# Gated DeltaNet layer: the sample's state scaling goes from GpSimd to ScalarE in pieces, the turn of the inverted blocks from ScalarE to VectorE

## The chip, the cores and the metric

The kernel runs on one core of a Trainium2 chip. The metric is device time in microseconds (us) of one launch, the median over several executions. A core has five instruction streams that run side by side and meet at semaphores: TensorE (PE in the profile; PEld are its weight loads), VectorE (DVE), ScalarE (ACT), GpSimd (POOL) and SyncE (SP), which here issues the DMAs. Each stream keeps its own order: an instruction that waits holds up all behind it on its engine.

## What is computed

One inference step of a trunk of two layers with 1024 channels: layer 0 mixes tokens by gated DeltaNet, layer 1 by RWKV-7. There is one prompt of 1024 tokens with 16 learned tokens ahead of it, and a batch of 8 samples of 8 tokens each that carry on from given states. Only the first layer matters here. Cut to that:

```
proj = rmsnorm(x) @ w_in                     # q, k, v, z, b, a
q, k, v = silu(causal_conv(q|k|v, last 3 rows))
q, k = l2norm(q) * 128**-0.5, l2norm(k)      # 8 key heads, each used by 2 of the 16 value heads
beta, g = sigmoid(b), -exp(a_log) * softplus(a + dt_bias)
# in chunks (64 tokens of the prompt, the 8 tokens of a sample), gc = cumsum(g):
A = I + strict_lower((beta k) k^T * decay)   # solved: u, w = A^-1 [beta v, beta k exp(gc)]
v_new = u - w S
o = (q exp(gc)) S + (tril(q k^T) * decay) v_new
S = S * exp(gc_last) + (k exp(gc_last - gc))^T v_new
y = (rmsnorm(o) * silu(z)) @ w_out ;  x = x + y
```

For the samples there are 8 states S of 128x128 for each of the 16 heads, 128 matrices in all. The new states `S * exp(gc_last) + ...` are an output (`out_s_gdn`).

## The kernel before, in words

**Groups.** The 16 value heads are done in 8 groups j = 0..7 of one key head and two value heads. All tokens (samples first, then prompt) stand in 9 tiles of 128, and three column pieces s = 0, 1, 2 of up to 408 columns go through the projection (`product`, matmuls `d..<-xc/xa,whi/wlo`). A weight tile is loaded (`wraw`), rounded by ScalarE into `whi` (L86), and GpSimd forms the remainder `wlo = wraw - whi` (L90); TensorE needs both. ScalarE and VectorE do the convolution (`raw`, `cvy`, `vt`, L523, L529, L543, L547).

**The inverse.** The blocks of a group's A are written to DRAM in 32x32 pieces (`ltd`, L715), read back with one block per partition (`invA`, L726), and inverted row by row on VectorE in 31 steps, each of a product `invtmp<-invA,invT` (L570) and a sum `invT<-invT,invtmp` (L572). `steps` deals these out between other work; `spread` (L737) runs what is left, then turns each inverted block (L740, 72 partitions by 1024 numbers, read with a stride of 32 numbers: `"p i j -> p j i"`) into `invA`, writes the turned blocks to DRAM as `g_u` (L742) and the unturned ones as `g_t` (L743), and reads them back: three DMAs `T1n<-g_t` (L746) and twelve `TT<-g_u` (L753). With `T1n`, TensorE starts the first of four merges (`y32`, matmuls `rY<-T1n,E`), which VectorE copies into `invA` (L764), and three more follow (`rU`, `rY`, `rU`). The write of `g_t` waits for the last inverse step, that of `g_u` for the turn, and both stand ahead of `T1n` in SP's queue.

**The chain.** `gdn_recur` walks over the 9 token tiles of the group: X (L877 to L880) and `rA<-X,TT`, then `w<-rA,nbp` on ScalarE (L62), `rA<-w,ktok` and `rA<-w,attn` on TensorE, S on VectorE (L902), `rA<-S,K` for the next tile, and o (ScalarE L62, VectorE L913). After three tiles the outputs are normalised: `ovar` (VectorE, L1045), `ors` (GpSimd, L102), `on_t` (VectorE, L110 to L112), and `o<-o,ors` on ScalarE (L62, 128x128, scale per partition).

**The sample's states.** For each head, four samples at a time, `sample_states` loads a tile `Sb` of 128x4x128 (L1076). `gdn_sample_scale` (L1098) multiplies the eight states of a head by their decay `eglb`, with one GpSimd instruction of 128x128 each (L1101). `gdn_sample_write` (L1103) adds the matmul results `msw` and `fsw` on VectorE (L1112) and stores the tile (L1113, `out_s_gdn`).

**What sets the order.** `gdn_events` files every piece of work under a slot number (one period of a group is 36 slots); `chain_events` files what belongs to a group's chain relative to the slot a at which the chain begins. TensorE's and ScalarE's instructions stand in the order of these slots. A scheduler orders VectorE, GpSimd and SP by its own estimates, so a change in one place can move other rows there. In the trace, groups 4 to 7 repeat with a period of about 124 us (from 582 us to about 1080 us); groups 0 to 3 lie ahead of that, with longer stretches of the inverse behind one another. Layer 1 follows from about 1260 us.

Of the kernel before, what the change touches and what calls it, by code (L numbers as in the profile page):

```python
# [10 lines left out]
AF = mybir.ActivationFunctionType  # L11
ALU = mybir.AluOpType
# [23 lines left out]
class Builder:  # L36
# [634 lines left out]
    def gdn_prep(self, j, G):  # L671

        nc, t, fp = self.nc, self.t, self.fp
# [58 lines left out]
        def steps(n):  # L732
            with self.tc.issue_after(self.anchor) if self.anchor else ExitStack():
                for _ in range(n):
                    next(G.inv, None)

        def spread():  # L737
            steps(31)
            A, Tv = buf[0][0:72, 0:1024], G.Tv
            nc.scalar.copy(G.Av, Tv.rearrange("p i j -> p j i"))  # L740
            ud, td = self.dram([72, 1024], f"g{j}_u"), self.dram([54, 1024], f"g{j}_t")
            nc.sync.dma_start(ud, A)  # L742
            nc.sync.dma_start(td, Tv[0:54].rearrange("p i j -> p (i j)"))  # L743
            T1 = self.T1n
            for r in range(3):
                nc.sync.dma_start(T1[32 * r:32 * r + 32, :, 32 * (r % 2):32 * (r % 2) + 32],  # L746
                                  td[18 * r:18 * r + 18].rearrange("c (i j) -> i c j", j=32))
            G.TT = [self.TTs[(3 * j + s) % 4] for s in range(3)]
            TT.extend(G.TT)
            for s in range(3):  # L750
                for r in range(4):
                    b = slice(32 * r, 32 * r + 32)
                    nc.sync.dma_start(G.TT[s][b, :, b], ud[18 * r + 6 * s:18 * r + 6 * s + 6].rearrange("c (j i) -> j c i", i=32))  # L753
# [181 lines left out]
    def at(self, u, f, *a):  # L935
        self.events.setdefault(u, []).append(lambda: f(*a))

    def chain_events(self, j, G, a):

        it, Sb, nm = [], {}, {}  # L940
        at = lambda u, *f: self.at(a + u, *f)

        def begin():
            it.append(self.gdn_recur(j, G[j]))
            next(it[0])

        def decay(s):
            if s == 0:
                G[j].at, G[j].kt, G[j].w = [None] * 3, [None] * 9, [None] * 9
            G[j].at[s] = self.decays(j, s, self.gp, "attn", 2)  # L950

        def exps(s, tt):
            self.decay_exps(j, s, G[j].at[s], tt)

        def scores(s):
            self.gdn_scores(j, s, G[j], G[j].at[s])

        def tokens(tg):
            G[j].kt[tg] = self.gdn_tokens(j, G[j], tg)

        def states(h):
            Sb[h] = [self.sample_states(j, h, q) for q in (0, 1)]

        def norm(s):
            nm[s] = self.gdn_norm(j, G[j], s, *G[j].seg[s])
        for s, (u, v, w) in enumerate(((-8.5, -5.6, -2.5), (1.6, 4.3, 6.5), (8.2, 10.3, 12.4))):
            at(u, decay, s)
            for tt in range(3):
                at(v + 0.9 * tt, exps, s, tt)
            at(w, scores, s)  # L970
        at(-4.3, states, 0)
        at(-3.4, lambda: self.gdn_sample_scale(j, 0, Sb[0]))
        at(-1.4, tokens, 0)
        at(-1, begin)
        for x in range(26):
            at(x, lambda: next(it[0]))
            if x % 3 == 1:
                at(x + 1.3, lambda: G[j].squares())
        for tg, u in enumerate((0.4, 3.6, 7.5, 10.5, 13.5, 16.5, 19.5, 22.5)):
            at(u, tokens, tg + 1)  # L980
        at(0.6, lambda: self.gdn_sample_rows(G[j], 0))
        at(2.2, lambda: self.gdn_sample_write(j, 0, G[j], Sb[0]))
        at(2.6, lambda: self.gdn_sample_rows(G[j], 1))
        at(2.7, states, 1)
        at(2.8, lambda: self.gdn_sample_scale(j, 1, Sb[1]))
        at(5.2, lambda: self.gdn_sample_write(j, 1, G[j], Sb[1]))
        for s in range(3):
            at(9 * s + 8.4, norm, s)
            for tt in range(3):
                at(9 * s + 10.2 + 0.5 * tt, lambda s=s, tt=tt: nm[s](tt))  # L990
            for h in (0, 1):
                at((14.5, 23.5, 30.5)[s] + h, lambda s=s, h=h: self.gdn_norm_out(j, G[j], s, h))
# [102 lines left out]
            for b in range(4):  # L1095
                self.nc.gpsimd.tensor_scalar(G.we[:, b], w[0:64], self.bmask4[:, b:b + 1], None, op0=ALU.mult)

    def gdn_sample_scale(self, j, h, Sb):  # L1098
        for g in (0, 1):
            for u in range(4):  # L1100
                self.nc.gpsimd.tensor_scalar(Sb[g][:, u], Sb[g][:, u], self.eglb[:, 2 * j + h, 4 * g + u:4 * g + u + 1], None, op0=ALU.mult)  # L1101

    def gdn_sample_write(self, j, h, G, Sb):  # L1103
        nc = self.nc
# [1437 lines left out]
```

## Time and profile before

| what | us |
|---|---|
| median of three runs | 2224.76 |
| the three runs | 2217.19, 2224.76, 2225.53 |
| the profiled execution | 2228.82 |
| its span in the profile | 2226.8 |
| busy in the span: TensorE, VectorE, ScalarE, GpSimd | 2070.8, 1580.8, 1270.7, 941.9 |
| mean granted TensorE clock | 0.971 |

The profile comes from one execution; 2.0 us of its time lie outside its span. Busy times are sums over an engine's instructions. A row of the timeline gives start, duration, engine, line, what is written from what, the shape and the count, and in brackets how long the engine had been idle and which event released it. A row of the waits gives who waited for whom, the sum, how often, and the longest. In a row of the windows stand, for one stretch, its length, then busy time and instruction count of PE, PEld, DVE, ACT and POOL, then the granted clock, the DMA share and GB/s. A row of a group ends with busy time, mean ns of one, and the idle time ahead of them with its commonest releaser.

### The profile page before, as it was taken

The numbers are of one execution on the slowest core, as the hardware profiler recorded it, in microseconds if no ns is written. First come the engines' busy times: TensorE is split into PE (matmuls) and PEld (weight loads), VectorE is DVE, ScalarE is ACT, GpSimd is POOL, SyncE is SP. The second block draws the span as 40 slices with busy tenths as digits, with TensorE's granted clock in tenths as the row PEclk, the third lists the DMA queues.
The fourth block names the chain that finished last, engine by engine and source line by source line (L and its number), as shares of the span: only waits on it lengthen the run. The fifth ranks groups of instructions, "written<-read, shape, count | busy, mean of one in ns | idle before, by whom it ended". The sixth has DMA issues, their size and how long they took to land. (4 is left out here: it accounts for less than half of the span.)

```text
span 2226.8 us, 54821 instructions
## 1 busy us (share of the span) xinstructions
PE 2070.8 (93%) x20404; PEld 1925.8 (86%) x20404; DVE 1580.8 (71%) x4213; ACT 1270.7 (57%) x3641; POOL 941.9 (42%) x1253
## 2 busy tenths in 40 slices
PE   5979898988999999999899999979899999999997
PEld 5879798888989998989799999968798988888886
DVE  6978868777786978776333585676887747876755
ACT  5436555555555555655633365674755546677774
POOL 3524435453354545444323154244533444444444
PEclk9989999998999999999999999989999999999999
DMA  4423242423333342434525314655566476677864
GB/s 117 117 67 104 67 113 81 104 75 85 99 107 81 88 115 79 104 93 114 169 78 142 86 49 152 221 165 177 163 184 170 122 211 170 191 218 231 237 176 137
DMA packets 430660, 292.64 MB, mean 131 GB/s; under 512 B 147145, under 2 KB 412986, under 8 KB 430394
## 3 DMA queue, kind: packets, MB, share of 16 engines
q1 hardware_dynamic: 430394, 289.14, 45.2%
q8 instruction: 161, 2.64, 0.5%
q14 instruction: 105, 0.86, 0.1%
HBM read 197.68 MB, written 91.37 MB: 130 GB/s over the span
## 5 line engine op out<-in xcount | busy, mean ns | idle before, releaser
L90 POOL TENSOR_TENSOR wlo<-wraw,whi 128x512 fp32r<-128x512 f32 (+1 forms) x246 | 322.4, 1312 | 381.6 <-ACT whi L86 335.0
L76 PE MATMUL d<-xc,whi 128*128 128x384 f32 (+2 forms) x1006 | 278.3, 336 | 1.1 <-DVE xc L312 0.7
L523 DVE SCALAR_TENSOR_TENSOR cvy<-raw,cw,cvy 128x408 f32<-128x408 f32 (+2 forms) x288 | 194.4, 676 | 31.6 <-ACT cvy L62 29.9
L86 ACT CAST whi<-wraw 128x512 fp32r<-128x512 f32 (+1 forms) x246 | 149.8, 611 | 94.6 <-PE d L76 50.5
L76 PEld LDWEIGHTS d<-xc,whi 128*128 128x128 f32 (+1 forms) x1006 | 182.6, 188 | 4.1 <-ACT whi L86 1.2
L76 PE MATMUL d<-xc,wlo 128*128 128x384 f32 (+3 forms) x476 | 157.0, 338 | 3.3 <-POOL wlo L90 3.3
L76 PE MATMUL dv<-xc,whi 128*128 128x384 f32 (+1 forms) x480 | 154.4, 341 | 0.0
L76 PE MATMUL dz<-xc,whi 128*128 128x384 f32 (+1 forms) x480 | 153.5, 338 | 0.0
L76 PE MATMUL d<-xa,whi 128*128 128x384 f32 (+3 forms) x450 | 141.1, 337 | 7.1 <-ACT ev L2342 4.3
L1101 POOL TENSOR_SCALAR Sb<-Sb,eglb 128x128 f32<-128x128 f32 x128 | 112.9, 898 | 74.2 <-DMA Sb<-in_state_gdn 33.9
L62 ACT ACTIVATE o<-rA,gcol 128x128 f32<-128x128 f32 x128 | 42.0, 367 | 132.8 <-DVE S L902 132.5
L570 DVE TENSOR_TENSOR invtmp<-invA,invT 72x31 f32<-72x31 f32 (+15 forms) x248 | 99.3, 400 | 3.4
L76 PE MATMUL dv<-xa,whi 128*128 128x384 f32 (+1 forms) x288 | 99.6, 346 | 0.0
L76 PE MATMUL dz<-xa,whi 128*128 128x384 f32 (+1 forms) x288 | 98.4, 342 | 0.0
L572 DVE TENSOR_TENSOR invT<-invT,invtmp 72x31 f32<-72x31 f32 (+15 forms) x248 | 95.6, 386 | 3.5
L76 PEld LDWEIGHTS d<-xc,wlo 128*128 128x128 f32 (+1 forms) x476 | 89.0, 188 | 7.0 <-POOL wlo L90 3.9
L76 PEld LDWEIGHTS dz<-xc,whi 128*128 128x128 f32 x480 | 89.3, 188 | 5.4 <-issue 5.3
L76 PEld LDWEIGHTS d<-xa,whi 128*128 128x128 f32 (+1 forms) x450 | 83.2, 188 | 11.0 <-ACT ev L2342 4.6
L76 PEld LDWEIGHTS dv<-xc,whi 128*128 128x128 f32 x480 | 90.7, 191 | 1.2 <-issue 1.2
L76 PE MATMUL d<-xa,wlo 128*128 128x384 f32 (+3 forms) x252 | 84.3, 334 | 1.1 <-POOL wlo L90 1.1
L76 PE MATMUL dq<-xc,whi 128*128 128x384 f32 (+1 forms) x240 | 80.2, 351 | 3.0 <-ACT whi L86 3.0
L76 PE MATMUL dk<-xc,whi 128*128 128x384 f32 (+1 forms) x240 | 79.3, 351 | 0.0
(523 smaller groups left out, 6881.6 us busy)
## 6 DMA issues: line engine op xcount, KB each, us to landing
wraw<-in_gdn_w_in SPq DMA_DIRECT2D x96, 256.0 KB
wraw<-in_rwkv_w_rkvz SPq DMA_DIRECT2D x80, 256.0 KB
Sb<-in_state_gdn SPq DMA_DIRECT2D x64, 256.0 KB
sldcak<-cakd SPq DMA_DIRECT2D x24, 576.0 KB
wraw<-in_rwkv_w_o SPq DMA_DIRECT2D x42, 256.0 KB
E<-drow SPq DMA_DIRECT2D x24, 384.0 KB
attn<-drow SPq DMA_DIRECT2D x24, 384.0 KB
wraw<-in_gdn_w_out SPq DMA_DIRECT2D x36, 256.0 KB
```

The costliest lines, as they stand in the source:

```text
L62: return self.nc.scalar.activation(out, in_, func, bias=bias, scale=scale, **kw)
L76: self.nc.tensor.matmul(out, lhsT, rhs, start=start, stop=stop)
L86: nc.scalar.copy(hi, x)
L90: e.tensor_tensor(lo, x, hi.bitcast(F32), op=ALU.subtract)
L523: nc.vector.scalar_tensor_tensor(y[0][:, 0:wd], raw[:, k:k + wd], cw[k], y[0][:, 0:wd], op0=ALU.mult, op1=ALU.add)
L570: nc.vector.tensor_tensor(tmp, A[:, j, j + 1:32].unsqueeze(2).broadcast_to([nb, n, m]), Tv[:, j, 0:m].unsqueeze(1).broadcast_to([nb, n, m] ...
L572: nc.vector.tensor_tensor(Tv[:, j + 1:32, 0:m], Tv[:, j + 1:32, 0:m], tmp, op=ALU.subtract)
L1101: self.nc.gpsimd.tensor_scalar(Sb[g][:, u], Sb[g][:, u], self.eglb[:, 2 * j + h, 4 * g + u:4 * g + u + 1], None, op0=ALU.mult)
```

## The change

Three edits:

1. In `spread`, the turn of the inverted blocks (L740) is a VectorE copy instead of a ScalarE copy. Shape and stride stay the same; there are 8, one for each group.
2. `gdn_sample_scale` takes a piece number k and scales two states of the head, half g = k // 2, with ScalarE (`act` with AF.Identity and a scale per partition) instead of all eight with GpSimd. There are 128 of these in all, as before.
3. The calls are filed as four pieces for each head, at slots a - 0.6, 0.3, 0.7 and 1.4 for the first head and a + 3.4, 3.8, 4.4 and 4.8 for the second, instead of all at a - 3.4 and a + 2.8.

```
-            nc.scalar.copy(G.Av, Tv.rearrange("p i j -> p j i"))
+            nc.vector.tensor_copy(G.Av, Tv.rearrange("p i j -> p j i"))
...
-        at(-3.4, lambda: self.gdn_sample_scale(j, 0, Sb[0]))
+        for k in range(4):
+            at((-0.6, 0.3, 0.7, 1.4)[k], lambda k=k: self.gdn_sample_scale(j, 0, Sb[0], k))
+            at((3.4, 3.8, 4.4, 4.8)[k], lambda k=k: self.gdn_sample_scale(j, 1, Sb[1], k))
...
-        at(2.8, lambda: self.gdn_sample_scale(j, 1, Sb[1]))
...
-    def gdn_sample_scale(self, j, h, Sb):
-        for g in (0, 1):
-            for u in range(4):
-                self.nc.gpsimd.tensor_scalar(Sb[g][:, u], Sb[g][:, u], self.eglb[:, 2 * j + h, 4 * g + u:4 * g + u + 1], None, op0=ALU.mult)
+    def gdn_sample_scale(self, j, h, Sb, k):
+        g = k // 2
+        for u in range(2 * (k % 2), 2 * (k % 2) + 2):
+            self.act(Sb[g][:, u], Sb[g][:, u], AF.Identity, scale=self.eglb[:, 2 * j + h, 4 * g + u:4 * g + u + 1])
```

GpSimd's queue in group 4, before: rows between two weight remainders. `Sb_8486` is the second half of the group's first head, `Sb_8828` the first half of its second head, `wlo_7979` the remainder of a weight tile of the next projection.

```order
L90 TENSOR_TENSOR wlo_7890<-wraw_7752,whi_7889 128x512
L511 COPY raw_7935<-raw_7859 128x3
L1101 TENSOR_SCALAR Sb_8486<-Sb_8486,eglb_124 128x128 x4
L505 MEMSET raw_8054 128x3
L1101 TENSOR_SCALAR Sb_8828<-Sb_8828,eglb_124 128x128 x4
L90 TENSOR_TENSOR wlo_7979<-wraw_7754,whi_7978 128x512
```

The same place of GpSimd's queue now:

```order
L90 TENSOR_TENSOR wlo_7890<-wraw_7752,whi_7889 128x512
L511 COPY raw_7935<-raw_7859 128x3
L505 MEMSET raw_8054 128x3
L90 TENSOR_TENSOR wlo_7979<-wraw_7754,whi_7978 128x512
L513 COPY last_6609<-raw_7935 128x3
```

The eight scalings between the two remainders are gone from this queue.

VectorE's queue at the end of the inverse of group 1, before: the last steps (`72x7x25` to `72x31`) and what stands behind them.

```order
L572 TENSOR_TENSOR invT_2237<-invT_2237,invtmp_2995 72x7x25
L570 TENSOR_TENSOR invtmp_2998<-invA_2235,invT_2237 72x156
L572 TENSOR_TENSOR invT_2237<-invT_2237,invtmp_2998 72x6x26
L570 TENSOR_TENSOR invtmp_3039<-invA_2235,invT_2237 72x135
L572 TENSOR_TENSOR invT_2237<-invT_2237,invtmp_3039 72x5x27
L570 TENSOR_TENSOR invtmp_3042<-invA_2235,invT_2237 72x112
L572 TENSOR_TENSOR invT_2237<-invT_2237,invtmp_3042 72x4x28
L570 TENSOR_TENSOR invtmp_3045<-invA_2235,invT_2237 72x87
L572 TENSOR_TENSOR invT_2237<-invT_2237,invtmp_3045 72x3x29
L570 TENSOR_TENSOR invtmp_3048<-invA_2235,invT_2237 72x60
L572 TENSOR_TENSOR invT_2237<-invT_2237,invtmp_3048 72x2x30
L570 TENSOR_TENSOR invtmp_3051<-invA_2235,invT_2237 72x31
```

The same queue now, its last rows up to the turn and the first merge's copy.

```order
L523 SCALAR_TENSOR_TENSOR cvy_3227<-raw_3159,cw_393,cvy_3227 128x384
L572 TENSOR_TENSOR invT_2237<-invT_2237,invtmp_3045 72x3x29
L529 SCALAR_TENSOR_TENSOR K_3278<-raw_3010,cvy_3126 128x64
L529 SCALAR_TENSOR_TENSOR K_3278<-raw_3010,cvy_3126 128x320
L523 SCALAR_TENSOR_TENSOR cvy_3227<-raw_3159,cw_393,cvy_3227 128x384
L570 TENSOR_TENSOR invtmp_3048<-invA_2235,invT_2237 72x60
L110 TENSOR_TENSOR on_t_3217<-ors_3216 128x6
L504 COPY raw_3961<-histT_2955 128x8x3
L523 SCALAR_TENSOR_TENSOR cvy_3227<-raw_3159,cw_393,cvy_3227 128x384
L572 TENSOR_TENSOR invT_2237<-invT_2237,invtmp_3048 72x2x30
L111 SCALAR_TENSOR_TENSOR on_t_3217<-on_t_3217,ovar_3214 128x6
L570 TENSOR_TENSOR invtmp_3051<-invA_2235,invT_2237 72x31
```

Before, the last seven steps stood behind one another without other work; now convolution (`cvy`, `K`), S, o and norm rows stand between them, and the last step (with L740 right behind it) comes after them. In this stretch the added rows ahead of the last step are six `cvy`, one `vt`, two S, two o, one `bv`, one `qeps`, one `ovar`, two `K`, three of the norm and one copy of `raw`.

ScalarE's queue in group 1, before: the turn stands ahead of the chain's `w`.

```order
L62 ACTIVATE raw_2826<-cvy_2902 128x384
L740 COPY invA_2235<-invT_2237 72x1024
L62 ACTIVATE ojunk_3080,ssq_2749<-o_2883 128x128
L62 ACTIVATE ojunk_3082,ssq_2749<-o_2883 128x128
L543 COPY raw_3010<-dk_3013 128x8x8
L544 COPY raw_3010<-dk_3013 128x320
L62 ACTIVATE w_3029<-rA_3031,nbp_544 128x128
```

And ScalarE's queue now, in group 4, about the second half of the second head (`Sb_8830`); in group 1 the rows above stand without the L740 row.

```order
L62 ACTIVATE Sb_8828<-Sb_8828,eglb_124 128x128 x2
L62 ACTIVATE o_8792<-rA_8797,gcol_123 128x128
L62 ACTIVATE o_8792<-rA_8798,gcol_123 128x128
L62 ACTIVATE E_8712<-E_8712,gcol_123 128x128 x2
L86 CAST whi_8909<-wraw_8679 128x512
L62 ACTIVATE attn_8770<-attn_8770,gcol_123 128x128 x2
L62 ACTIVATE Sb_8830<-Sb_8830,eglb_124 128x128 x4
L62 ACTIVATE E_8712<-E_8712,gcol_123 128x128 x2
```

The four scalings of this half stand between products of decays (`E`, `attn`) on ScalarE, behind the rounding `whi_8909`; before, they stood on GpSimd right ahead of the remainder of that same tile. In groups 4 to 7 VectorE's order ahead of the last inverse step is as before, and L740 stands one `cvy` behind that step. TensorE's order is the same up to the layer's output projection (about 1060 us), where GpSimd, VectorE and SP rows move among one another too.

## Prediction

> **What bounds the kernel now.** The page first, for the engines and the groups that the change touches.
>
> ```profile
> PE 2070.8 (93%) x20404; PEld 1925.8 (86%) x20404; DVE 1580.8 (71%) x4213; ACT 1270.7 (57%) x3641; POOL 941.9 (42%) x1253
> L1101 POOL TENSOR_SCALAR Sb<-Sb,eglb 128x128 f32<-128x128 f32 x128 | 112.9, 898 | 74.2 <-DMA Sb<-in_state_gdn 33.9
> ```
>
> TensorE is the bound at 93%, so an edit on other engines can win only what TensorE stands idle, and the time it runs at half clock. The windows say where that is: groups 0 to 3 in one stretch, then one row for each period.
>
> ```profile
> 60.00:582.00 522.00, 471.40 (x3956) 446.39 (x3956) 408.92 (x1132) 275.90 (x870) 222.38 (x335) 0.95 0.34 93
> 582.00:707.00 125.00, 119.31 (x1024) 113.04 (x1023) 95.93 (x278) 71.69 (x230) 58.57 (x82) 0.99 0.35 95
> 957.00:1082.00 125.00, 115.50 (x991) 108.16 (x990) 85.43 (x222) 73.10 (x240) 59.91 (x82) 0.99 0.42 117
> ```
>
> Groups 0 to 3 leave 522.0 - 471.4 = 50.6 us of TensorE idle and run at a clock of 0.95; a period of the later groups leaves 125.0 - 119.3 = 5.7 us. TensorE's waits name the releasers, first for 60 to 582 us (four rows), then for 582 to 1082 us (two).
>
> ```profile
> PE rY L76 <- DMA T1n<-g_t: 11.2, 5, 10.0
> PE rA L76 <- ACT w L62: 7.5, 1, 7.5
> PE dv L76 <- POOL wlo L90: 6.2, 2, 4.1
> PE f L73 <- DVE vt L529: 4.3, 2, 2.6
> ...
> PE rA L76 <- DVE S L902: 9.2, 8, 2.1
> PE dv L76 <- POOL wlo L90: 7.1, 4, 1.8
> ```
>
> In the later periods it waits once for GpSimd's `wlo` (7.1 us in 4 waits), and most of its waits for S, 9.2 us in 8 with 2.1 the longest, is one wait a period of about 2 us. In the earlier groups it waits for the read of the inverse (`T1n`), once for ScalarE's `w`, twice for `wlo` (4.1 and the remaining 2.1).
>
> **Scalings off GpSimd: the wait for wlo in groups 4 to 7.** GpSimd's rows of group 4, and TensorE's row behind them.
>
> ```profile
> 626.87 4.24 POOL L1101 TENSOR_SCALAR Sb<-Sb,eglb 128x128 f32<-128x128 f32 x4 [1.68 <-PE mktok L73]
> 631.14 4.20 POOL L1101 TENSOR_SCALAR Sb<-Sb,eglb 128x128 f32<-128x128 f32 x4
> 635.31 1.29 POOL L90 TENSOR_TENSOR wlo<-wraw,whi 128x512 fp32r<-128x512 f32 x1
> ...
> 636.65 0.44 PE L76 MATMUL dv<-xc,wlo 128*128 128x384 f32 x1 [1.76 <-POOL wlo L90]
> ```
>
> Eight scalings hold `wlo` until 635.31. Without these 8.4 us it can start 8 us sooner, and the wait of 1.76 us goes whatever else happens. The inverse's steps and S behind it wait for TensorE there, so they come earlier with it. Four periods: -7.0 us.
>
> **The wait for S at the period's end.** GpSimd, SP, VectorE and TensorE, in that order.
>
> ```profile
> 692.10 2.35 POOL L1101 TENSOR_SCALAR Sb<-Sb,eglb 128x128 f32<-128x128 f32 x4 [6.71 <-DVE X L880]
> 694.40 1.32 POOL L90 TENSOR_TENSOR wlo<-wraw,whi 128x512 fp32r<-128x512 f32 x1
> 710.07 1.32 POOL L102 TENSOR_TENSOR ors<-ovar,cvals 128x6 f32<-128x6 f32 x1
> ...
> 695.75 0.39 SPq L425 DMA_DIRECT2D wraw<-in_gdn_w_in  x1
> 699.59 1.12 SPq L1076 DMA_DIRECT2D Sb<-in_state_gdn  x2
> 704.42 0.44 SPq L646 DMA_DIRECT2D attn<-drow  x1
> ...
> 711.43 0.17 DVE L110 TENSOR_TENSOR on_t<-ors 128x6 f32<-128x6 f32 x1 [5.12 <-POOL ors L102]
> ...
> 712.32 0.49 PE L76 MATMUL rA<-S,K 128*128 128x128 f32 x2 [1.99 <-DVE S L902]
> ```
>
> The other four scalings hold the next `wlo` by up to 2.35 us; SP's next weight load waits for that `wlo` to free its buffer (695.75), and behind it in SP's queue stand the stores and loads of the states, `ltd` and `attn<-drow` (704.42). That last transfer feeds GpSimd's rows up to `ors` (710.07), VectorE waits 5.12 us for `ors` with S queued behind, and TensorE waits 1.99 us for S. Take the scalings away and the queue is up to 2.35 us early. The bounds are 0 (the stores of the states wait for ScalarE instead, or a landing of another transfer comes last) and 2.0; since the whole length of this chain moves and I see one link (the landing of the states' store ahead of 699.59) that needn't move, I take 1.0 each: -4.0 us, ends 0 and -8.
>
> Behind that wait the clock falls, behind the wait for `wlo` it doesn't (rows: after the first, then after the second).
>
> ```profile
> 638.00:642.00 4.00, 4.00 (x29) 4.00 (x28) 2.38 (x10) 2.54 (x7) 0.39 (x2) 1.00 0.62 180
> 714.00:718.00 4.00, 4.00 (x18) 4.00 (x17) 3.80 (x11) 3.94 (x17) 1.28 (x1) 0.57 0.25 65
> ```
>
> 18 matmuls instead of 29 in 4 us at a clock of 0.57: 4 x (1 - 0.57) = 1.7 us of work lost in a period. A wait of 1.76 us left the clock whole and one of 1.99 didn't; two rows so close set no safe edge for the 1 us that I leave standing, so I take half of the four: -3.4 us, ends 0 and -6.8. The Trainium skill ("TensorE: Matmul & The Clock Gate", Part 1) has the clock halved after an idle window of about 3.4 us, on windows that run free of the kernel's own times. By it alone the phase decides in each period, and the term could be either end; that two almost equal waits ended differently here agrees with it.
>
> **What ScalarE takes on.** The nearest rows are its own 128x128 scalings with a scale per partition, and the copy that it gives up.
>
> ```profile
> L62 ACT ACTIVATE o<-o,ors 128x128 f32<-128x128 f32 x144 | 48.4, 397 | 23.5 <-DVE ors L112 23.4
> L740 ACT COPY invA<-invT 72x1024 f32<-72x1024 f32 x8 | 16.5, 2065 | 28.2 <-DVE invT L572 28.2
> ```
>
> 128 scalings at 48.4 / 144 = 0.34 us of busy time are 43 us, 16.5 us go: +26.5 us on an engine that is busy 71.7 of 125 us in a period. Each place takes 0.7 to 1.4 us. Two of a group's four tiles were there at 626.87 already; the last is scaled on GpSimd from 692.10 and stands in ScalarE's queue behind a rounding and products of decays, so ScalarE shouldn't stand long for it. Behind the pieces in its queue are `w`, `zg` and `whi`, for which TensorE and VectorE wait. I cost this at nothing because ScalarE has over 50 us idle in a period; if that cover fails at one piece a period, it is 0.7 us x 8 = +5.6 us at most.
>
> **The turn on VectorE.** No row shows this copy there. Bounds: contiguous and strided transposes of 1024 numbers on VectorE.
>
> ```profile
> L1646 DVE STREAM_TRANSPOSE invA<-sGD x5: 1197/1245/1247, 1518.4 to 1729.8; 128x1024 f32<-128x1024 f32 x5
> L1653 DVE STREAM_TRANSPOSE T1n<-invT x5: 2039/2082/2105, 1556.6 to 1765.7; 128x1024 f32<-128x1024 f32 x5
> L878 DVE TENSOR_SCALAR X<-bv x16: 224/224/1230, 101.6 to 1023.8; 64x128 f32<-64x128 f32 x16
> ```
>
> I take 1.25 us, ends 0.7 (224 ns for 128 numbers leaves room for less than the contiguous row) and 2.1. The copy holds up `g_u` only; `T1n` waits for the landing of `g_t`. In group 1 `g_t` is issued at 258.36 and `T1n` from 261.19 (rows below), so 2.8 us hide the copy in every group: cost nothing, up to +0.5 us for each of the first four if it takes 2.1 and meets GpSimd. On that, L878's longest is 1230 ns against 224. The Trainium skill ("SBUF — State Buffer", Who interferes with whom) says that a copy or `tensor_scalar` on VectorE that uses both ports blocks GpSimd for its whole length and is blocked by it; the spread of L878 agrees. By it the copy could end one `wlo` (1.3 us) later, 1.25 + 1.3 = 2.55 us, an estimate, still under 2.8.
>
> **Groups 0 to 3: a wait exchanged for another.** Group 1: ScalarE, TensorE, VectorE's last steps, SP, TensorE; then SP and TensorE in group 0.
>
> ```profile
> 258.37 1.93 ACT L740 COPY invA<-invT 72x1024 f32<-72x1024 f32 x1 [10.30 <-DVE invT L572]
> 261.78 1.23 PE L76 MATMUL rA<-w,ktok 128*128 128x128 f32 x4 [7.48 <-ACT w L62]
> ...
> 254.53 0.33 DVE L572 TENSOR_TENSOR invT<-invT,invtmp 72x175 f32<-72x175 f32 x1
> 258.15 0.19 DVE L572 TENSOR_TENSOR invT<-invT,invtmp 72x31 f32<-72x31 f32 x1
> 262.54 0.64 DVE L523 SCALAR_TENSOR_TENSOR cvy<-raw,cw,cvy 128x408 f32<-128x408 f32 x1 [4.20 <-ACT cvy L62]
> ...
> 258.36 0.27 SPq L743 DMA_DIRECT2D g_t<-invT  x1
> 261.19 1.49 SPq L746 DMA_DIRECT2D T1n<-g_t  x3
> ...
> 268.15 1.33 PE L76 MATMUL rY<-T1n,E 32*32 32x32 f32 x72
> ...
> 135.06 0.29 SPq L743 DMA_DIRECT2D g_t<-invT  x1
> ...
> 140.82 0.28 PE L76 MATMUL rY<-T1n,E 32*32 32x32 f32 x2 [9.99 <-DMA T1n<-g_t]
> ```
>
> ScalarE stood 10.30 us at the turn and TensorE 7.48 us for the `w` behind it. That goes. But VectorE's queue now has some twenty more instructions ahead of the last step: six `cvy` at 0.64 us (the row of 262.54), 3.8 us, and fourteen others (`vt`, `bv`, two `K`, two S, two o and six small ones) that lie between the 0.17 us of `on_t` above and about 0.5; at 0.28 they are 3.9 us, 7.7 in all. The last steps took 258.15 - 254.53 = 3.6 us, so the inverse ends at about 254.5 + 3.6 + 7.7 = 265.8 instead of 258.3. From the issue of `g_t` to the start of `rY` group 0, where TensorE waits for nothing else, takes 140.82 - 135.06 = 5.8 us, so `rY` can start at 271.6. Before it started at 268.15. So TensorE saves 7.48 us at `w` and waits about 11 us at `rY`: **+3.5 us**, with ends of -2 (VectorE's rows find their inputs early and overlap) and +8 (they wait for the matmuls `dk`, for `ors` or for GpSimd's port).
>
> Group 0 already waits 9.99 us there; three `cvy` and one `vt`, 3 x 0.64 + 0.3 = 2.2 us, now stand ahead of its last steps: +2. In group 2 the `wlo` wait of 2.1 us goes, in group 3 that of 4.1 us and the wait of 2.6 us for `vt`, but the end of the inverse takes their place, since convolution rows stand ahead of it there too: I keep -2 of 8.8 us for group 2 and -1 for group 3. Together: +2.5 us, ends -12 and +15.
>
> **The sum.** -7.0 - 4.0 - 3.4 + 2.5 = -11.9 us, rounded to -12. Layer 1 and the output projection keep their work; rows move there among one another, which I hold to ±3. Against the profiled execution's 2228.8 us this is 2216.8. That execution is 4.1 us above the median of 2224.8, itself within runs 8.3 us apart; the same difference on the median gives **2212.8 us**, 0.54% less. A measurement of this kernel can tell about 0.5%, 11 us.
>
> **The rivals.**
> *More goes than I take.* S waits and their clock losses vanish in all four periods (-8 and -6.8), and groups 0 to 3 come out even or gain as the clock recovers: 2224.8 - 22 to -30, about 2200. For it: all four periods show the same chain, with 2.35 us held and 2.0 us waited. Against it: a freed link usually meets the next.
> *Only wlo.* The S wait stays, as the landings set it: -7.0 + 2.5 = -4.5, 2220. For it: VectorE's wait for `ors` is 5.12 us long, and one late transfer keeps it.
> *The inverse becomes the bound, slower.* VectorE's queue in groups 0 to 3, at the last steps: the rows dealt in ahead of them wait for ScalarE, TensorE and GpSimd in turn, so that the inverse ends over 10 us later than before in groups 1, 2 and 3. Once the delay in a group exceeds the wait that goes there (7.5, 2.1 and 6.7 us), each further us is lost: +2, +8, +6 and +6 give 22, less 7 to 11 from the later periods: +11 to +15, about 2237. For it: VectorE is busy 409 of 522 us there, and `on_t` now waits for `ors` ahead of the last step. Against it: ScalarE, freed 10 us sooner, feeds those rows earlier.
> *Nothing moves in sum.* The freed GpSimd time is hidden and ScalarE's pieces delay `w` or `zg` by as much: 2225 ± 4. Against it is the 1.76 us wait, which has one releaser in all four periods.
>
> **How the numbers follow.** Forecast 0.40 (own range 2206 to 2219), more goes 0.20, only wlo 0.20, slower 0.13, nothing 0.07. Faster by over 0.5%: 0.22 of the forecast's 0.40, and all of the second, 0.42; slower by over 0.5%: 0.10 of the fourth's 0.13; the rest, 0.48, within. The range leaves out about 1 in 10 at each end: 2197 to 2231.
>
> **What would show it.** Right: no `wlo` wait near 636, 761, 884 and 1008; S waits under 1 us and fewer half-clock stretches; ScalarE's L62 group with 128 more rows near 0.34 us; VectorE's copy between 0.7 and 2.1 us; in group 1 no `w` wait but 8 to 14 us at `rY`. Wrong: S waits of 2 us remain; `rY` waits of over 3 us in each of groups 1 to 3; TensorE waiting behind a ScalarE scaling.

## The result and the profile after

The changed kernel takes 2211.69 us (median of 12 runs, 2202.76 to 2221.03) against 2224.57 us (12 runs, 2217.19 to 2232.51). The ratio is 0.9942, with a 95% interval of 0.9922 to 0.9962: 13 us faster, where 12 were forecast. The two profiled executions, 2228.82 and 2211.06 us, lie 17.8 us apart; the runs spread over 15 us before and 18 now.

The page of the changed kernel, first its engines, then the two groups that moved.

```profile
PE 2061.5 (93%) x20404; PEld 1918.4 (87%) x20404; DVE 1587.6 (72%) x4221; ACT 1291.1 (58%) x3761; POOL 838.3 (38%) x1125
...
L62 ACT ACTIVATE Sb<-Sb,eglb 128x128 f32<-128x128 f32 x128 | 43.5, 398 | 1.2 <-DMA Sb<-in_state_gdn 1.2
...
L740 DVE COPY invA<-invT 72x1024 f32<-72x1024 f32 x8 | 8.7, 1084 | 0.1
```

The work went where the diff puts it: 128 scalings on ScalarE for 43.5 us, which stood only 1.2 us for their loads, and eight copies on VectorE at 1.08 us. The windows say where time came from.

```profile
60.00:582.00 522.00, 467.10 (x3961) 444.40 (x3960) 405.44 (x1137) 286.88 (x930) 175.74 (x274) 0.94 0.34 93
582.00:707.00 125.00, 123.06 (x1065) 117.03 (x1064) 103.40 (x299) 79.31 (x262) 44.74 (x67) 1.00 0.36 97
957.00:1082.00 125.00, 114.78 (x1000) 106.56 (x999) 84.79 (x206) 81.81 (x293) 46.81 (x65) 0.99 0.47 136
```

TensorE's idle time in 125 us of a later period fell from 5.7 to 1.9 us and the clock there is whole; in the stretch of groups 0 to 3 it rose from 50.6 to 54.9 us. (In the third row the changed kernel is over 16 us ahead, so other work stands in it than before.) A stretch with the same work in both kernels is the one from the first merge of group 4 to that of group 7, three periods with 3060 matmuls. Before, then now:

```profile
648.98:1020.88 371.90, 356.30 (x3060) 338.02 (x3059) 294.90 (x836) 215.82 (x692) 171.60 (x243) 0.99 0.36 97
641.50:1000.09 358.59, 351.75 (x3061) 333.07 (x3060) 298.19 (x840) 223.26 (x737) 132.88 (x197) 1.00 0.37 101
```

Idle time fell from 15.6 to 6.8 us. Busy time fell by 4.6 us too: matmuls take longer where the clock is halved (the prediction's rows have 18 in 4 us at a clock of 0.57, 29 at 1.00), and the three half-clock stretches that lay there before (from 714.4, 837.3 and 960.1 us, 3.4 us each) are gone. The waits of TensorE, for 60 to 582 us and then for 582 to 1082 us, put names to this.

```profile
PE rY L76 <- DMA T1n<-g_t: 35.7, 7, 11.8
PE mhist L73 <- DVE zg L1064: 3.6, 1, 3.6
...
PE rA L76 <- DVE o L913: 4.9, 11, 0.8
PE f L73 <- DMA stage<-in_x_prompt: 4.0, 2, 3.2
PE rA L76 <- DVE S L902: 2.2, 5, 1.0
```

No wait for `wlo` is left in the later periods and little for S; `w` and `wlo` are gone from the earlier ones, and the wait for the read of the inverse has grown from 11.2 to 35.7 us.

The chain that set S at a period's end, in GpSimd, SP, VectorE (to be read against the rows from 692 to 712 us before):

```profile
685.36 1.27 POOL L90 TENSOR_TENSOR wlo<-wraw,whi 128x512 fp32r<-128x512 f32 x1 [7.00 <-ACT whi L86]
699.71 1.33 POOL L102 TENSOR_TENSOR ors<-ovar,cvals 128x6 f32<-128x6 f32 x1
...
686.66 0.39 SPq L425 DMA_DIRECT2D wraw<-in_gdn_w_in  x1
690.65 1.12 SPq L1077 DMA_DIRECT2D Sb<-in_state_gdn  x2
691.86 1.91 SPq L715 DMA_DIRECT2D ltd<-E  x4
693.82 0.44 SPq L646 DMA_DIRECT2D attn<-drow  x1
...
701.08 0.17 DVE L110 TENSOR_TENSOR on_t<-ors 128x6 f32<-128x6 f32 x1 [1.41 <-POOL ors L102]
```

`wlo` itself comes when its `whi` is ready and not behind the scalings. Counted from the group's first merge (at 648.98 us before, at 641.50 now), it starts after 43.9 us instead of 45.4, and `ors` after 58.2 instead of 61.1. VectorE waits 1.41 us for `ors` instead of 5.12, and S no longer holds TensorE.

Group 1: VectorE's last step and the turn, SP, TensorE.

```profile
263.18 0.19 DVE L572 TENSOR_TENSOR invT<-invT,invtmp 72x31 f32<-72x31 f32 x1
263.40 1.02 DVE L740 COPY invA<-invT 72x1024 f32<-72x1024 f32 x1
...
263.40 0.28 SPq L743 DMA_DIRECT2D g_t<-invT  x1
266.24 1.40 SPq L746 DMA_DIRECT2D T1n<-g_t  x3
...
268.71 0.28 PE L76 MATMUL rY<-T1n,E 32*32 32x32 f32 x2 [11.83 <-DMA T1n<-g_t]
```

TensorE came to `rY` at 256.9, ahead of the inverse's end at 263.4, and stood there 11.83 us.

A measure that all runs below share is where in the trace a group's first merge (`rY`) starts. Period is a third of the way from group 4 to group 7. Each mark comes from one execution; where a kernel was traced twice (e4 and e10, e7 and e11), the period differs by up to 0.5 us and the marks by up to 3. Behind group 7's merge an execution can lose more: e1's traced one took 2213.05 us, its median is 2197.69.

| kernel | ratio to before (95%) | `rY` of group 4, against before | period | `rY` of group 7, against before |
|---|---|---|---|---|
| before | 1 | 648.98 us | 123.97 | 1020.88 us |
| changed | 0.9942 (0.9922 to 0.9962) | -7.5 | 119.53 | -20.8 |
| e1 scalings only | 0.9875 (0.9847 to 0.9904) | -22.7 | 119.06 | -37.4 |
| e2 turn only | 1.0053 (1.0031 to 1.0076) | +6.9 | 124.31 | +8.0 |
| e3 changed, last tile on GpSimd | 1.0037 (1.0014 to 1.0061) | +1.5 | 123.66 | +0.6 |
| e4 changed, inverse early | 0.9844 (0.9818 to 0.9869) | -28.9 | 119.77 | -41.5 |
| e5 changed, old slots | 1.0226 (1.0205 to 1.0246) | +30.9 | 127.30 | +40.9 |
| e6 last tile only | 0.9948 (0.9930 to 0.9965) | -8.6 | 119.28 | -22.7 |
| e7 e1, inverse early | 0.9804 (0.9787 to 0.9821) | -32.6 | 118.45 | -49.2 |
| e8 changed, scaled twice | 0.9953 (0.9936 to 0.9970) | -6.2 | 119.67 | -19.1 |

### The profile page after: what moved, and what is told of

Its sections match the earlier page's. It is cut to its first block, busy times and chain, and to the rows that moved or that the text cites. A ratio compares the mean times of both kernels' runs of the same rounds, so it can differ in the third digit from the quotient of the medians.

```text
span 2209.3 us, 54820 instructions
## 1 busy us (share of the span) xinstructions
PE 2061.5 (93%) x20404; PEld 1918.4 (87%) x20404; DVE 1587.6 (72%) x4221; ACT 1291.1 (58%) x3761; POOL 838.3 (38%) x1125
## 3 DMA queue, kind: packets, MB, share of 16 engines
q1 hardware_dynamic: 430394, 289.14, 45.4%
## 5 line engine op out<-in xcount | busy, mean ns | idle before, releaser
L76 PEld LDWEIGHTS d<-xa,whi 128*128 128x128 f32 (+1 forms) x450 | 84.6, 191 | 10.3 <-ACT ev L2343 3.5
L62 ACT ACTIVATE mixs<-xb,omu 128x64 f32<-128x64 f32 (+3 forms) x128 | 61.7, 521 | 18.9 <-DVE xc L90 8.2
```

The costliest lines, as they stand in the source:

```text
L62: return self.nc.scalar.activation(out, in_, func, bias=bias, scale=scale, **kw)
L76: self.nc.tensor.matmul(out, lhsT, rhs, start=start, stop=stop)
```

## The experiments

**The two halves apart.** e1 leaves the turn on ScalarE; e2 is the kernel before with the turn alone moved.

```
# e1, on the changed kernel
-            nc.vector.tensor_copy(G.Av, Tv.rearrange("p i j -> p j i"))
+            nc.scalar.copy(G.Av, Tv.rearrange("p i j -> p j i"))
# e2, on the kernel before: the same line the other way round
```

> Only the scalings go to ScalarE in pieces; the turn stays a ScalarE copy. My theory (the later periods gain by the scalings leaving GpSimd, the turn edit costs in group 1 and wins little elsewhere): groups 4 to 7 gain about 4 us a period as in the changed kernel, so no wlo wait of 1.8 us and no S wait of 2 us there; in group 1 TensorE again waits about 7.5 us for w behind the turn and not at rY; total 10 to 18 us below before. Rival (ScalarE freed of the turn is what brings the gain, the scalings on GpSimd were hidden): waits and total as before, within 4 us.

> Only the turn goes to VectorE; the scalings stay whole on GpSimd at their old slots. My theory: groups 4 to 7 keep their waits of 1.8 us for wlo and about 2 us for S with the half clock behind it, group 1 waits about 11 us at rY in place of 7.5 us at w; total 0 to 6 us above before. Rival (the turn brings the gain): total 10 us or more below before, S waits gone.

e1 is 28 us faster than before, more than was expected, e2 12 us slower, also more: 0.9875 x 1.0053 = 0.9927, near the 0.9942 of both together. So one half of the change gains and the other costs about 15 us. TensorE's waits from 60 to 582 us, two rows of e1 and two of e2:

```profile
PE rY L76 <- DMA T1n<-g_t: 10.9, 4, 10.0
PE rA L76 <- ACT w L62: 7.5, 1, 7.5
```

```profile
PE rY L76 <- DMA T1n<-g_t: 26.5, 7, 11.9
PE dv L76 <- POOL wlo L90: 7.4, 3, 4.1
```

With the turn on ScalarE the wait of 7.5 us for `w` stays and `rY` waits for little beyond group 0's 10; with the turn on VectorE it is the other way round, as the theory said. In the later periods e2 keeps both old waits (`rA` for S 10.3 us in 8, `wlo` 7.1 in 4):

```profile
PE rA L76 <- DVE S L902: 10.3, 8, 2.8
PE dv L76 <- POOL wlo L90: 7.1, 4, 1.8
```

The rival, that freeing ScalarE of the turn brings the gain, falls. Of e2's four S waits of 2 us only the first two are followed by half clock, to which the account below comes back.

**Which wait counted in the later periods.** e3 puts the last of a group's four tiles back on GpSimd; e6 moves that tile alone.

```
# e3, on the changed kernel (e6: the kernel before, with the branches exchanged and the slots -3.4, 2.8 for the other three tiles)
-            at((3.4, 3.8, 4.4, 4.8)[k], lambda k=k: self.gdn_sample_scale(j, 1, Sb[1], k))
+            at((3.4, 3.8, 2.8, 2.8)[k], lambda k=k: self.gdn_sample_scale(j, 1, Sb[1], k))
...
+            if h and g:
+                self.nc.gpsimd.tensor_scalar(Sb[g][:, u], Sb[g][:, u], self.eglb[:, 2 * j + h, 4 * g + u:4 * g + u + 1], None, op0=ALU.mult)
+            else:
                 self.act(Sb[g][:, u], Sb[g][:, u], AF.Identity, scale=self.eglb[:, 2 * j + h, 4 * g + u:4 * g + u + 1])
```

> The changed kernel with the last of a group's four tiles (second head, second half) scaled on GpSimd again at its old slot. My theory of two separate waits: the wlo wait of 1.8 us stays away, the S wait of about 2 us and the half clock behind it come back in each later period, so groups 4 to 7 gain about 1.8 us a period instead of 4.1 and the total is 6 to 10 us above the changed kernel. Rival (the S wait went because everything upstream of it came earlier, not because of this tile): S waits stay under 1 us and the total is the changed kernel's within 3 us.

> Before, with only the last of a group's four tiles on ScalarE; the other three tiles stay on GpSimd and the turn on ScalarE. My theory by now (the S wait bounds the later periods; taking the wlo wait away alone gave 0.3 us a period): the wlo wait of 1.8 us stays, the S wait and its half clock go, a later period falls from 124.0 to between 120.5 and 121.5 us, total 8 to 18 us below before. Rival (neither wait counts unless both go): the period stays above 123 us. Second rival (the last tile carries all): the period falls to 119.5 us and the wlo wait is hidden in it.

In e3 the wait for `wlo` stays away and the S wait is back, with the half clock behind it (GpSimd, TensorE, then the window behind it):

```profile
694.65 2.35 POOL L1103 TENSOR_SCALAR Sb<-Sb,eglb 128x128 f32<-128x128 f32 x4 [7.29 <-DMA Sb<-in_state_gdn]
696.96 1.30 POOL L90 TENSOR_TENSOR wlo<-wraw,whi 128x512 fp32r<-128x512 f32 x1
...
714.89 0.49 PE L76 MATMUL rA<-S,K 128*128 128x128 f32 x2 [2.19 <-DVE S L902]
...
716.00:720.00 4.00, 4.00 (x18) 4.00 (x17) 3.33 (x11) 4.00 (x15) 1.28 (x1) 0.57 0.19 45
```

That decides between the two theories for the place of the S wait, but the size was missed: I expected the period to keep 1.8 us of gain, and it is 123.66 against 123.97 us. The whole kernel is about 21 us slower than the changed one where 6 to 10 were expected. e6 shows the other side. One tile on ScalarE takes the period to 119.28 us, while eight scalings still stand ahead of `wlo` and TensorE still waits for it, though less (0.88 instead of 1.76 us):

```profile
747.54 0.44 PE L76 MATMUL dv<-xc,wlo 128*128 128x384 f32 x1 [0.88 <-POOL wlo L90]
```

So the second rival of e6 came true: the last tile carries nearly all of the gain in the later periods. The way from its `wlo` to `ors` is as long in e6 as before (15.5 and 15.7 us in group 4), but it begins earlier: this `wlo` starts 42.7 us behind the group's first merge in e6, 45.4 before and 46.5 in e3, and `ors` 58.2, 61.1 and 62.1 us behind it, within 1 us of that in the next two periods too. That the delay goes through SP's queue is read from the rows; no run moves a link of that queue alone.

The wait of 1.76 us at `wlo` was worth 0.3 us a period (e3 against before; 0.65 against e2, which has the turn on VectorE too) and 0.2 (e1, 119.06, against e6), at the edge of what one trace tells. Where the rest went shows in the stretch from group 4's merge to group 7's, here for e2, e3 and e6:

```profile
655.91:1028.85 372.94, 354.25 (x3060) 335.03 (x3060) 300.26 (x840) 210.15 (x689) 175.35 (x245) 1.00 0.35 97
650.49:1021.48 370.99, 357.57 (x3060) 337.57 (x3059) 301.66 (x840) 219.77 (x725) 138.26 (x209) 0.99 0.36 97
640.39:998.22 357.83, 350.48 (x3060) 333.53 (x3060) 293.42 (x832) 219.19 (x704) 166.11 (x231) 1.00 0.37 101
```

From e2 to e3 idle time falls from 18.7 to 13.4 us, by all of the three `wlo` waits (5.3 us), but busy time rises by 3.3 us: each of e3's three S waits there is followed by half clock, and of e2's only the first. Against before, other waits take back 3.1 of the 5.3 us (those of `mog`, a matmul that reads the outputs, for ScalarE's `o` 1.6, for S 0.6, for VectorE's `o` 0.5, for `vt` 0.4), and busy time rises by 1.3. In e6, against before, idle time falls by 8.2 us, of which the waits for S give 5.6 (6.9 to 1.3) and those for `wlo` 2.7 (5.3 to 2.6), and busy time by 5.8, with the half clock gone. The shorter wait at `wlo` goes with the second four scalings, which take 3.07 us there instead of 4.20; why they are quicker is open.

The other three tiles do count in groups 1 to 3: e1 lies 14.1 us ahead of e6 at group 4's merge.

**What the turn costs, and why.** e4 and e7 let the inverse's steps of groups 1 to 3 stand ahead of the chain's latest X or S row (`self.anchor`) on VectorE; e4 has the turn on VectorE, e7 on ScalarE.

```
-            with self.tc.issue_after(self.anchor) if self.anchor else ExitStack():
+            with self.tc.issue_after(self.anchor) if self.anchor and j not in (1, 2, 3) else ExitStack():
```

> The changed kernel, but the inverse's steps of groups 1 to 3 need not wait for the latest S row on VectorE, which puts the last step 27 and 28 VectorE rows earlier in groups 1 and 3. My theory (the waits of 11.8 and 9.7 us at rY are the late end of the inverse in VectorE's order): they fall by 5 us or more each and the total falls 5 to 14 us below the changed kernel. Rival (the rows dealt in ahead only fill VectorE while TensorE is ahead anyway; taken out, they come late and TensorE waits for X, S or vt instead): rY waits shorter, but as much waiting in other rows, total within 3 us of the changed kernel.

> The scalings on ScalarE, the turn left on ScalarE, and the inverse's steps of groups 1 to 3 free of the wait for the latest S row. Theory (the turn on VectorE costs by the order of VectorE's rows alone): with the order mended the engine of the turn is worth little, total within 5 us of the kernel with the turn on VectorE and the early inverse (0.984 of before). Rival (the copy's own time on VectorE, or ScalarE's stand at the turn, counts): more than 6 us faster, or more than 6 us slower, than that kernel.

In e4 the waits at `rY` in groups 1 and 3 are gone; what is left is group 0's:

```profile
PE rY L76 <- DMA T1n<-g_t: 11.7, 2, 11.2
PE rA L76 <- DVE o L913: 3.9, 9, 0.8
PE rA L76 <- DVE S L902: 3.5, 2, 1.7
```

It gained about 22 us on the changed kernel (0.9844 against 0.9942), above the 5 to 14 expected: the half clock behind those two waits is gone as well, which the trace of the changed kernel has for 17.1 us from 259.6 and 13.7 us from 512.2. The rows that were dealt in ahead of the last step did come later, and TensorE hardly waits for them (S 3.5 us). So the late end of the inverse in VectorE's order is shown to be the loss at those two waits.

e7 is faster still, 0.9804, about 9 us ahead of e4, and the best kernel here. By its expectation that is the rival: the place of the turn counts for itself. How much of the loss each makes shows at group 4's merge: the turn on VectorE stands 15.2 us behind the turn on ScalarE without this edit (changed against e1) and 3.7 us with it (e4 against e7). So some 11 us there are the late inverse. The edit also brings e7 about 16 us against e1, whose ScalarE stood at the turn for that same inverse.

To see what the place of the turn costs, I made the copy twice on VectorE (e9, otherwise e4's kernel); e10 is e4's kernel and e11 is e7's once more, on the same chip.

```
             nc.vector.tensor_copy(G.Av, Tv.rearrange("p i j -> p j i"))
+            nc.vector.tensor_copy(G.Av, Tv.rearrange("p i j -> p j i"))
```

> The kernel with the scalings on ScalarE, the early inverse and the turn on VectorE, with the turn's copy made twice (1.1 us more on VectorE in each group, into the same place). If the copy's own time on VectorE is what makes the turn dearer there than on ScalarE (7.7 us at the start of the last group's merge in the two profiles): about as much again, 5 us or more later at that point and 5 us or more in the total. If it is only rows that stand in another order in group 0 and a later placing: within 3 us of the single copy at that point.

> The single copy on VectorE with the early inverse once more, on the same chip as its two neighbours, for their comparison: 0.982 to 0.987 of before.

> The same with the turn on ScalarE once more: 0.978 to 0.983 of before, 5 to 12 us faster than the kernel with the turn on VectorE.

Ratios: twice 0.9893 (0.9867 to 0.9918), once 0.9851 (0.9828 to 0.9875), on ScalarE 0.9815 (0.9789 to 0.9842). Group 7's merge starts at 989.9, 980.2 and 974.4 us. A second copy costs about 9 us in all, of the size of what the first costs, 8 us, against ScalarE; the intervals of neighbours overlap a little, but no run of one of these kernels lies among the runs of another, and both marks stand in the same order. In the later periods each copy on VectorE adds about 1 us, its own time: a period is 118.4 us with none, 119.3 with one (119.8 in e4) and 120.3 with two. Ahead of them it isn't so even: of the 9.8 us by which e9 is behind e10 at group 7's merge, 7.1 arise between the merges of groups 1 and 2, and which rows moved there I did not trace. So the copy's own time is shown to count in groups 4 to 7, and time and order are not separated in groups 0 to 3.

**The pieces.** e5 files the ScalarE scalings at the old slots.

```
-            at((-0.6, 0.3, 0.7, 1.4)[k], lambda k=k: self.gdn_sample_scale(j, 0, Sb[0], k))
-            at((3.4, 3.8, 4.4, 4.8)[k], lambda k=k: self.gdn_sample_scale(j, 1, Sb[1], k))
+            at(-3.4, lambda k=k: self.gdn_sample_scale(j, 0, Sb[0], k))
+            at(2.8, lambda k=k: self.gdn_sample_scale(j, 1, Sb[1], k))
```

> The changed kernel with its ScalarE scalings filed at the old slots (each head's eight together, ahead of products of decays, w and whi) instead of in pieces. If the pieces matter: ScalarE stands 3 us or more a period for the load of the last tile, with zg and w queued behind it, TensorE waits for w, zg or S, and a later period is at least 1.5 us longer than the 119.5 us of the changed kernel; total 6 us or more above it. If only the engine matters: later periods within 0.5 us and total within 4 us of the changed kernel.

It is 50 us slower than before. ScalarE, then TensorE:

```profile
723.52 1.28 ACT L62 ACTIVATE Sb<-Sb,eglb 128x128 f32<-128x128 f32 x4 [10.80 <-DMA Sb<-in_state_gdn]
725.66 0.60 ACT L62 ACTIVATE w<-rA,nbp 128x128 f32<-128x128 f32 x2
...
726.06 1.22 PE L76 MATMUL rA<-w,ktok 128*128 128x128 f32 x4 [6.49 <-ACT w L62]
```

ScalarE stands 10.80 us for the load of the last tile with `w` queued behind, and TensorE 6.49 us for `w`. Before, GpSimd stood 6.71 us at this place, which held up one remainder and S behind it by 2 us; on ScalarE, whose order is fixed by hand, it holds up the chain itself. Scalings in pieces on GpSimd were not run, so what the filing alone does there is open.

**ScalarE's cover.** e8 adds to each scaling a second ScalarE instruction on the same data, into a scratch tile.

```
+            self.act(self.t(self.gp, [128, 128], "ojunk", 1, BF16), Sb[g][:, u], AF.Identity)
```

> The changed kernel with each of the 128 ScalarE scalings followed by another ScalarE instruction of 128x128 into a scratch tile, which adds about 0.3 us each, 38 to 43 us of ScalarE time. Theory (ScalarE's time there is covered): no new wait of TensorE above 1 us, a later period within 1 us of 119.5 us, total within 5 us of the changed kernel. Rival (ScalarE's queue ahead of w, zg and whi is the next bound): a later period 2 us or more longer, total 10 us or more above.

```profile
L62 ACT ACTIVATE Sb<-Sb,eglb 128x128 f32<-128x128 f32 x128 | 50.0, 391 | 0.9 <-DMA Sb<-in_state_gdn 0.9
L62 ACT ACTIVATE ojunk<-Sb 128x128 bf16<-128x128 f32 x128 | 39.7, 310 | 3.7
```

About 46 us more on ScalarE (39.7, and 50.0 instead of 43.5) lengthen a period by 0.14 us, less than two traces of one kernel differ, and the total stays within the changed kernel's interval (0.9953 against 0.9942). ScalarE's time at these places is covered.

## Why the prediction was right, and where its steps were not

The total was right: -12 forecast, -12.9 measured. That it came within 1 us is in part luck, since the terms were off by more and in both directions. In the profiled pair groups 0 to 3 came out 3.6 us better than forecast, the four later periods about 5 us better and what lies behind them 3.3 us worse, and this pair lies 17.8 us apart where the medians lie 12.9.

**The wait for `wlo`, -7.0: wrong.** The step said that the 1.76 us go "whatever else happens", and counted all of them as gain. The wait did go, but e2, e3, e1 and e6 show that it brought 0.2 to 0.7 us a period, 1 to 3 us in four: other waits of TensorE and the half clock behind S took the rest, as the stretches above show.

**The S wait and the clock, -4.0 and -3.4: right in place, about half of what came.** e6 gives -4.7 us a period for this tile alone: 1.9 us less waiting for S (1.0 forecast), 1.9 us less busy time with the half clock gone (0.85 forecast) and 0.9 us at `wlo`, which the forecast had in the other term. Both S and clock came out at about their outer ends (2.0 and 1.7): in e6 the chain starts 2.8 us earlier behind the merge, more than the 2.35 us of scalings that stood ahead of it, and of the four half-clock stretches from 582 to 1078 us before none is left, not half. The caution about the clock was right all the same. A wait of 1.51 us for S (before, at 835.88 us) was followed by half clock, while waits of 1.87 and 1.86 us (e2, at 845.35 and 968.87 us) were not, so the length of the wait alone doesn't decide. In SP's rows the four `ltd` issues ahead of `attn<-drow` took 3.58 us before and take 1.91 now, but such a long issue stands in two of the four periods only, and all four had the S wait.

The two errors nearly cancel: the forecast was -14.4 us for four periods, 3.6 each, and three measured at -4.4 each.

**What ScalarE takes on: right.** 43 us forecast, 43.5 measured, at no cost, and e8 shows the cover. It rests on the pieces: e5.

**The turn on VectorE, "cost nothing": wrong.** The duration was right (1.25 taken, 1.08 measured), and the cover of 2.8 us for `g_u` held: `T1n` was issued 2.84 us after `g_t`. But the cost isn't in `g_u`; it is in VectorE's queue. With the inverse early, the place on VectorE costs some 8 us in all (e10 against e11), about 1 us of it in each later period, and e2 puts the whole move at +12.

**Groups 0 to 3, +2.5: the waits as told, the sum not.** In group 1 the wait for `w` is gone and 11.83 us stand at `rY` for the 11 forecast. Its second merge started 4.5 us later than before (+3.5 forecast), but by another way than the forecast had it: the inverse ended at 263.4, not 265.8, `rY` itself started only 0.6 us later than before, and the other 4 us are the half clock behind that wait (17.1 us from 259.6), for which the forecast had no term. Group 0's merge came 0.8 us later, not 2. From matmul to matmul, groups 2 and 3 gave back 2.2 and 3.3 us (2 and 1 forecast), so that at 582 us the changed kernel stood 1.1 us ahead, not 2.5 behind. The rival that the inverse becomes the bound was half true: it held TensorE in groups 1 and 3 (1.7 us in group 2), and the turn on VectorE took about 15 us there (e1 against changed at group 4's merge), some 11 of them by the late inverse. The gain of the scalings in the same groups just paid for that. I had not seen that gain, since I took the inverse as the bound there in both cases.

**The rest, ±3.** From group 7's merge to the end 3.3 us of the profiled pair's gain were lost, among them a wait of 3.2 us for a load of `stage` (1.6 at the same place before). What of that is the change and what is the spread from run to run, I didn't separate.

## What to carry to other kernels

A wait that shows in the waits is worth only what the next wait, or the clock behind it, doesn't take back: move one cause alone (e3, e6) before adding up the waits. An instruction that waits for a load must stand behind that load's landing in a queue whose order is made by hand, or all behind it waits (e5 against the changed kernel, 63 us). And two edits that come together should be run apart: half of this change was worth 28 us, the other half cost about 15, and with the inverse's steps let go earlier the first half alone comes to 0.9804 of before.

## What the runs showed of the hardware

The copy on VectorE and instructions on GpSimd hold each other up. In e9, the two copies of one group and GpSimd's rows:

```profile
621.54 1.12 DVE L740 COPY invA<-invT 72x1024 f32<-72x1024 f32 x1
624.15 2.20 DVE L741 COPY invA<-invT 72x1024 f32<-72x1024 f32 x1
```

```profile
623.77 1.61 POOL L90 TENSOR_TENSOR wlo<-wraw,whi 128x512 fp32r<-128x512 f32 x1
626.42 0.95 POOL L560 MEMSET invT<- 72x1024 f32 x1 [1.04 <-DVE invA L741]
```

The second copy starts inside the running `wlo` and ends 626.35 - 625.38 = 0.97 us behind its end; alone it takes 1.0 to 1.1 us. In the five of eight groups where it met a running `wlo` it took 2.0 to 2.2 us, in the other three 1.03 to 1.08. The Trainium skill ("SBUF — State Buffer", Who interferes with whom) states such a lock for copies that use both of VectorE's ports, and the estimate of a copy held up by one remainder that the prediction made from it has the right size. The single copy of the changed kernel met no running `wlo`: it took 1.13 us at most.

The other way round, in e9's group 1, VectorE first, then GpSimd there and in group 3:

```profile
252.97 1.07 DVE L740 COPY invA<-invT 72x1024 f32<-72x1024 f32 x1
```

```profile
253.09 1.02 POOL L519 COPY last<-raw 128x24 f32<-128x24 f32 x1 [5.23 <-DVE hist L487]
496.48 0.21 POOL L519 COPY last<-raw 128x24 f32<-128x24 f32 x1 [4.89 <-ACT raw L543]
```

GpSimd's small copy of 128x24, 0.21 us in group 3, took 1.02 us where it started inside VectorE's copy, and ended 0.07 us behind it.

The same strided 72x1024 copy takes 1.08 us on VectorE and 2.07 us on ScalarE.
